# Block gates of two channel tiles in one run of products, and loaded tiles read later in the plan

## The chip, the cores and the metric

The kernel runs on one core of one Trainium2 chip. The metric is device time of one execution, in microseconds (us). Engines: TensorE (PE in the profile, its weight loads PEld) multiplies; VectorE (DVE), ScalarE (ACT) and GpSimd (POOL) work on elements; SyncE (SP) issues nearly all DMAs. Each engine takes its instructions in the order in which the program lists them.

## The reference

One encoder layer on 512 tokens of width 1024, in float32:

```python
h = rms_norm(x, g_pre) * (1 + scl) + shift            # scl, shift, gate from silu(c) @ w_c + b_c
xa, za, q, k, v, zb, ga, gb = split(h @ w_in)         # eight parts of 1024 columns
xa = centred_dwconv(xa, conv_w, conv_b)               # 4 taps along the sequence
h_fwd = rg_lru(xa, w_r_f, ...)                        # r, i = sigmoid(block_diag(xa)), 16 blocks of 64
h_bwd = rg_lru(xa, w_r_b, ..., reverse=True)          # linear recurrence along the sequence
y_a = ((h_fwd + h_bwd) * silu(za)) @ w_pa
y_b = (neighbourhood_attention(q, k, v, rpb) * silu(zb)) @ w_pb
merged = sigmoid(ga) * y_a + sigmoid(gb) * y_b
out = rms_norm(x + gate * (merged @ w_o), g_final)
```

## The kernel before

**Products.** A float32 product is made of three products of rounded parts: each operand is split into a high part (a cast on ACT, `whi`) and a remainder (a subtraction on DVE or POOL, `wlo`), and `mm3` (line 383) multiplies high by high, high by low and low by high into one PSUM bank. One output tile of 128 channels x 512 tokens is one call of `proj` (line 684): a 512 KB load `wraw` on SP, the cast `whi`, the subtraction `wlo`, and 8 steps of 3 matmuls, 24 in all. Here p*n* stands for the *n*-th of them; the list `main` keeps the first matmul of each, and a load is held back until p(*n*-5) has begun.

**Stages.** First the products for v, written out to a scratch in memory (`vscr`) and read back in pieces (`vt`). Then 8 pairs of heads, three products each (q, k, z), with the attention of a pair threaded between products: scores (`sp`), a bias step on DVE with a row minimum (`ttr`, line 799), exponentials on ACT (line 806), transposes on TensorE (`pt`, line 813), their split into parts (`pp`: ACT line 819, DVE line 821), the product with v (`pv`, line 829), and the combination of its parts (`vp`, `yt`: lines 838 to 844). Then four groups *g* of two channel tiles for the recurrent branch. Then eight merging products with `w_pa`, and the output product with `w_o` and the final norm.

**A group**, tiles 2g and 2g+1, is eight products: two for xa, two for za, two for ga, two with `w_pb`. After an xa product, `conv_gates` (line 930) makes the convolution `xc` (ACT, then three DVE steps), its parts `xh` and `xl`, and then the gates of this tile in one PE step, "gates" (line 954): 12 matmuls that use 64 rows of the array each, in 6 pairs, one pair member on the rows 0 to 63 and one on the rows 64 to 127, into four PSUM banks of class `gt`. ACT empties each bank in two halves (tanh, lines 960 and 963), DVE makes `ix` (line 968). `gate_a` (line 972) makes silu of za. `recur` (line 979) does the rest of the recurrence for both tiles and both directions: on ACT `dec` (line 986), `th` (line 988) and a square root (line 993), on DVE two products and a scan (lines 998 to 1005), the sum, the product with za, and the parts `yah`, `yal`, which the merging products read.

**Who sets the order.** Nothing is issued directly. `Plan.run` (line 258) is a list scheduler that runs when the kernel is built. Every `op` has a cost in us, a rank and its dependencies; the plan keeps a modelled time for each engine, and takes on each engine, among the steps that could begin within a small window of the earliest one (`WIN`, line 101), the one of lowest rank (line 280). It models the eight PSUM banks with a limit for each class (`LIMITS`, line 32), the tile slots in SBUF (36 of 512 columns, 32 of 1024) and the landing of DMAs (line 222). `late` (line 239) is added to the time at which a step's successors may begin in the plan. The order that comes out is the order of instructions on each engine; the planned times themselves are not kept. On the chip an engine whose next instruction has to wait holds up all that is behind it.

Of the kernel before, what the change touches and what calls it, by code (L numbers as in the profile page):

```python
# [28 lines left out]

NS, NW = 36, 32  # L30
WARM = 60
LIMITS = {"hx": 8, "acc": 3, "sp": 4, "pt": 2, "pv": 2, "mi": 2, "hd": 3, "gt": 4}


BLOCKS = [(0, 24, 8), (8, 32, 0), (24, 32, 0), (40, 24, 0)]
# [60 lines left out]
class Plan:  # L96
# [15 lines left out]
    def fixed(self, ap):  # L112
        return Tile_(None, ap=ap)

    def op(self, eng, cost, fn, rank, r=(), w=(), rw=(), lock=False, after=(), spare=0, size=0, until=None, late=0.0, hold=(), name=""):
        o = Op()
        o.alts = {eng: cost} if isinstance(eng, str) else dict(zip(eng, cost))
        o.fn, o.rank, o.lock, o.spare, o.size, o.name = fn, rank, lock, spare, size, name
        o.n, o.until, o.late = len(self.ops), until, late
        deps = set()  # L120
        for t in list(r) + list(rw):
            for f in t.family():
                deps.update(f.writers)
        for t in list(w) + list(rw):
            for f in t.family():
                deps.update(f.readers)
        for t in r:
            t.readers.append(o)
        for t in w:
            t.writers.append(o)  # L130
        for t in rw:
            for f in [t] + t.parts:
                f.writers, f.readers = [], []
            t.writers = [o]
        o.tiles = list(dict.fromkeys(t.base or t for t in list(w) + list(rw) + list(r) + list(hold)))
        for t in o.tiles:
            t.uses += 1
        o.data, o.succ, o.t = set(deps), [], 0.0
        deps.update(after)
        o.left = len(deps)  # L140
        for d in deps:
            d.succ.append(o)
        self.ops.append(o)
        return o
# [113 lines left out]
    def run(self):  # L258
        self.free = {e: 0.0 for e in self.ENG}
        self.dma, self.dve, self.pool = 0.0, 0.0, 0.0  # L260
        self.lanes = [0.0] * 8
        self.idle = [o for o in self.ops if o.until is not None]
        self.ready = {e: [] for e in self.ENG}
        for o in self.ops:
            if o.left == 0:
                self.enter(o)
        n = 0
        while n < len(self.ops):
            best = None
            for e in self.ENG:  # L270
                cand = []
                for _, _, o in self.ready[e][:40]:
                    s = self.est(o, e)
                    if s is not None and o.until is None:
                        cand.append((s, o))
                        if s <= self.free[e]:
                            break
                if cand:
                    lim = min(s for s, _ in cand) + self.WIN[e]
                    s, o = next(c for c in cand if c[0] <= lim)  # L280
                if self.idle and e == "PE":
                    f = self.idle[0]
                    fs = self.est(f, e)
                    if fs is not None and f.left == 0 and (not cand or fs + f.alts[e] <= s):
                        s, o, cand = fs, f, [f]
                if not cand:
                    continue
                if best is None or s < best[0]:
                    best = s, e, o
            if best is None:  # L290
                raise RuntimeError("nothing can begin: " + ", ".join(
                    f"{e}: {[(round(r, 2), o.name) for r, _, o in self.ready[e][:4]]}" for e in self.ENG))
            s, e, o = best
            for f in o.alts:
                self.ready[f].remove((o.rank, o.n, o))
            if self.idle and o is self.idle[0]:
                self.idle.pop(0)
            self.commit(o, e, s)
            n += 1
            if self.idle and o is self.idle[0].until:  # L300

                for d in self.idle:
                    self.ready[e].remove((d.rank, d.n, d))
                    self.leave(d)
                n += len(self.idle)
                self.idle = []
# [23 lines left out]
def layer(ctx, tc, x, x_t, par, w_m, w_g, bc_gate, w_v, w_in, w_blk, rpb, amask, w_pa, w_pb, w_o, g_final, out):  # L330
# [8 lines left out]
    def op(eng, cost, fn, rank, name="", **kw):  # L339
        return pl.op(eng, cost, fn, HEAD.get(name, rank), name=name, **kw)  # L340
# [27 lines left out]
    def load(t, dst, src, rank, size, after=(), spare=0, r=(), late=0.0, name="load"):  # L368

        return op("SP", 0.45, lambda e: nc.sync.dma_start(dst(), src() if callable(src) else src), rank,  # L370
                  r=r, w=[t], after=after, spare=spare, size=size, late=late, name=name)

    def cast(o, i):

# [306 lines left out]
    def gate_of(n, back):  # L681
        return [main[max(0, n - back)]] if n - back >= 0 else []

    def proj(w, rh, rl, lo="DVE"):

        n = len(main)
        raw, hi, low = W("wraw"), W("whi", F32R), W("wlo", F32R)
        v = lambda t: (lambda: t.ap.rearrange("p (k c) -> p k c", k=KD))
        load(raw, whole(raw), w, n - 5, 524288, after=gate_of(n, 5), spare=1,
             name=f"w{n}")  # L690
        op("ACT", act(1024), cast(whole(hi), whole(raw)), n - 2.2, r=[raw], w=[hi], after=gate_of(n, 3), name=f"whi{n}")
        engs = (lo,) if isinstance(lo, str) else lo
        costs = [dve(1024) if e == "DVE" else pool_(1024) for e in engs]
        op(engs, costs, sub(whole(low), whole(raw), whole(hi)), n - 2.1, r=[raw, hi], w=[low], lock=True, name=f"wlo{n}")
        o = B("acc")
        for k in range(KD):
            def f(e, k=k):
                mm3(o.ap, v(hi)()[:, k, :], v(low)()[:, k, :], rh[k][1](), rl[k][1](), k == 0, k == KD - 1)
            first = op("PE", pe(512, 3), f, 1000 + n + 0.01 * k, r=[hi, low, rh[k][0], rl[k][0]], rw=[o], name=f"p{n}")
            if k == 0:  # L700
                main.append(first)
        return n, o


# [50 lines left out]
    def attention(pr, q, k, z, nbt, pos):  # L755
# [24 lines left out]
        def half(bs):  # L780
# [79 lines left out]
        op("PE", 0.15, lambda e: nc.tensor.transpose(rcb.ap[:8, :P], rc.ap, ident.ap), pos - 0.3, r=[rc, ident], w=[rcb], name="rcb")  # L860
        op("ACT", 0.3, lambda e: nc.scalar.activation(rct.ap[:8, :P], rcb.ap[:8, :P], AF.Copy, scale=0.5), pos - 0.3, r=[rcb], w=[rct],
           name="rct")
        op("SP", 0.5, lambda e: nc.sync.dma_start(scr.ap, rct.ap[:8, :P]), pos - 3, r=[rct], w=[scr], size=4096, name="rcs")
        for h in range(2):
            src = bass.AP(scr.ap.tensor, scr.ap.offset + h * P, [[0, 64], [2 * P, 4], [1, P]])
            load(rcx, lambda h=h: rcx.ap[H[h], :].rearrange("p (b q) -> p b q", b=4), src, pos - 3, 131072, r=[scr], name="rcl", late=1.0)
# [60 lines left out]
        op("ACT", act(512), cast(whole(hi), whole(raw)), pos - 1, r=[raw], w=[hi], name="gwh")  # L927
        op("DVE", dve(512), sub(whole(lo), whole(raw), whole(hi)), pos - 1, r=[raw, hi], w=[lo], lock=True, name="gwl")

    def conv_gates(i, xa):  # L930
        n, o = xa
        xc = T("xc")
        op("ACT", act(512, 2), lambda e: nc.scalar.activation(xc.ap, o.ap, AF.Identity, bias=pc(64 + i, 65 + i),
# [8 lines left out]
        xh, xl = T("xh", F32R), T("xl", F32R)  # L942
        op("ACT", act(512), cast(whole(xh), whole(xc)), n, r=[xc], w=[xh], name="xh")
        op("DVE", dve(512), sub(whole(xl), whole(xc), whole(xh)), n, r=[xc, xh], w=[xl], lock=True, name="xl")
        g, c0 = gw[i // 2], (i % 2) * 256
        ri = [T("ri") for _ in range(4)]
        bks = [[B("gt"), B("gt")] for _ in range(2)]

        def f(e_):
            for d in range(2):  # L950
                for m, (w, xx) in enumerate(((g[0], xh), (g[0], xl), (g[1], xh))):
                    for e in range(2):
                        mm(bks[d][e].ap, w.ap[H[e], c0 + d * P:c0 + (d + 1) * P], xx.ap[H[e], :], m == 0, m == 2)
        op("PE", 1.55, f, n + 0.5, r=[g[0], g[1], xh, xl], w=bks[0] + bks[1], name="gates")
        for d in range(2):
            bk = bks[d]
            c = 16 * d + i
            for e in range(2):
                def f0(e_, e=e, d=d, bk=bk, c=c):
                    nc.scalar.activation(ri[2 * d].ap[H[e], :], bk[e].ap[H[e], :], AF.Tanh, bias=hb.ap[H[e], c:c + 1], scale=0.5)  # L960

                def f1(e_, e=e, d=d, bk=bk, c=c):
                    nc.scalar.activation(ri[2 * d + 1].ap[H[e], :], bk[e].ap[H[1 - e], :], AF.Tanh,
                                         bias=hb.ap[H[1 - e], c + 8:c + 9], scale=0.5)
                op("ACT", act(512, 1), f0, n + 0.3, r=[bk[e], hb], w=[ri[2 * d]], name="gr")
                op("ACT", act(512, 1), f1, n + 0.3, r=[bk[e], hb], w=[ri[2 * d + 1]], name="gi")
            u = ri[2 * d + 1]
            op("DVE", dve(512), lambda e, u=u: nc.vector.scalar_tensor_tensor(u.ap, u.ap, 1.0, xc.ap, op0=ALU.add, op1=ALU.mult),
               n + 0.6, r=[xc], rw=[u], lock=True, name="ix")
        st[i] = ri  # L970

    def gate_a(i, z):
        n, o = z
# [57 lines left out]
    for g in range(4):  # L1031
        tiles = (2 * g, 2 * g + 1)
        n0 = len(main)
        ybv = lambda: ([(ybh[k], whole(ybh[k])) for k in range(KD)], [(ybl[k], whole(ybl[k])) for k in range(KD)])
        load_gates(g, n0, gate_of(n0, 3))
        for i in tiles:
            conv_gates(i, proj(w_in[i], hhl, hll))
        for i in tiles:
            gate_a(i, proj(w_in[8 + i], hhl, hll))
        recur(tiles, n0 + 10)  # L1040
        for i in tiles:
            gate_m((i, 0), proj(w_in[48 + i], hhl, hll))
        for i in tiles:
# [241 lines left out]
```

## Time and profile before

| | |
|---|---|
| runs, us | 566.6, 566.64, 568.99; median 566.64 |
| the profiled execution | 569.44 us; its span, first to last instruction, 567.6 us; 1.84 us lie around it |
| mean granted clock of TensorE | 0.995 |
| ACT busy, DVE busy, POOL busy | 57%, 68%, 18% of the span |
| DMA | 83.47 MB, 147 GB/s on average |

The profile is of one execution, which was 2.8 us longer than the median of the runs. Times in it are us from the span's start; the durations of groups are means in ns. The busy time of PE is modelled from overlapping matmuls: one matmul of 512 columns shows some 0.39 us, while the next one starts 0.23 us after it. So what PE loses is read from the distance of starts, not from the busy share. The rows that the prediction works with stand in it.

### The profile page before, as it was taken

Reading aid. Unit: us, or ns where it says so; the run is one execution under the profiler, and the core shown is the slowest. Engines: PE = TensorE matmul, PEld = TensorE weight load, DVE = VectorE, ACT = ScalarE, POOL = GpSimd, SP = SyncE. Lnnn points to the kernel's source line nnn. Section 1 sums busy time; section 2 is a strip of 40 time slices with the busy share of each in tenths; the row PEclk is TensorE's granted clock in tenths of the full one; section 3 lists DMA queues with packets and bytes.
Section 4 is the critical chain, followed back from the end, with each engine's and each line's share of the span. In section 5 each row is a group of like instructions: output and inputs, shape, how many; then the busy total and the mean of one; then the engine's idle time right before and its main releaser. Section 6 shows DMA issues by size and latency. Waiting matters only on the chain.

```text
span 567.6 us, 7658 instructions
## 1 busy us (share of the span) xinstructions
PE 555.9 (98%) x2781; PEld 459.3 (81%) x2781; DVE 388.4 (68%) x696; ACT 322.4 (57%) x568; POOL 100.7 (18%) x95
## 2 busy tenths in 40 slices
PE   8999997999999999999999999999999999999995
PEld 8788886888888888887887887787788888888885
DVE  5899754665576667886489559749847996398323
ACT  6442545557466557579938867984894433234133
POOL 1103539184454550000000000000000000000220
PEclk9999998999999999999999999999999999999999
DMA  8993896652824721305222222223239813380002
GB/s 303 410 401 97 316 270 190 188 148 62 256 56 116 219 88 64 130 13 210 82 104 94 93 83 103 75 74 112 74 106 320 278 38 112 116 329 1 1 37 112
DMA packets 35580, 83.47 MB, mean 147 GB/s; under 512 B 3615, under 2 KB 10967, under 8 KB 35543
## 3 DMA queue, kind: packets, MB, share of 16 engines
q1 hardware_dynamic: 35264, 82.66, 44.1%
q8 instruction: 22, 0.36, 0.3%
q10 hardware_dynamic: 279, 0.32, 0.2%
q14 instruction: 15, 0.12, 0.1%
HBM read 76.65 MB, written 6.32 MB: 146 GB/s over the span
## 4 chain that ended last, share of the span: by engine, by line
PE 89%; DMA 7%; SPq 2%; DVE 1%; ACT 1%; issue 0%; ACTq 0%
PE acc L381 74%; PE hx L381 6%; DMA wv<-in_w_v_dram 3%; PE pv L381 3%; PE gt L381 2%; PE pt L813 2%; PE sp L381 2%; DMA vt<-vscr 2%; DMA wraw<-in_w_in_dram 1%; SPq L370 1%; DMA xT<-in_x_t_dram 1%; SPq L675 1%; DVE va L672 0%; DVE vl L378 0%; ACT vh L375 0%
## 5 line engine op out<-in xcount | busy, mean ns | idle before, releaser
L381 PE MATMUL acc<-hhl,whi 128*128 128x512 f32 x784 | 247.2, 396 | 0.0
L381 PEld LDWEIGHTS acc<-hhl,whi 128*128 128x128 f32 x784 | 143.8, 189 | 30.1 <-issue 1.8
L381 PE MATMUL acc<-hhl,wlo 128*128 128x512 f32 x392 | 153.5, 392 | 0.0
L381 PEld LDWEIGHTS acc<-hhl,wlo 128*128 128x128 f32 x392 | 73.9, 188 | 16.1
L375 ACT CAST whi<-wraw 128x1024 fp32r<-128x1024 f32 x72 | 74.2, 1045 | 9.1 <-DMA wraw<-in_w_in_dram 8.1
L378 POOL TENSOR_TENSOR wlo<-wraw,whi 128x1024 fp32r<-128x1024 f32 x23 | 56.5, 2457 | 73.2 <-ACT whi L375 39.0
L378 DVE TENSOR_TENSOR wlo<-wraw,whi 128x1024 fp32r<-128x1024 f32 x49 | 59.3, 1220 | 14.2 <-ACT whi L375 13.7
L1151 POOL TENSOR_TENSOR yo<-yo,gfin 128x512 f32<-128x512 f32 x6 | 8.2, 1360 | 338.0 <-ACT xr L1148 338.0
L381 PE MATMUL acc<-woh,mhl 128*128 128x512 f32 (+1 forms) x144 | 40.4, 365 | 0.0
L381 PE MATMUL acc<-yahl,whi 128*128 128x512 f32 x128 | 39.4, 389 | 0.0
L381 PE MATMUL acc<-ybhl,whi 128*128 128x512 f32 x128 | 39.4, 389 | 0.0
L1028 DVE SCALAR_TENSOR_TENSOR gm<-gm,acc 128x512 f32<-128x512 f32 x16 | 11.0, 688 | 39.4 <-PE acc L381 39.4
L799 DVE CUSTOM_DVE_ANT_0 p<-sp,nb 128x192 f32<-128x192 f32 (+1 forms) x64 | 32.7, 610 | 6.1 <-PE sp L381 6.1
L730 POOL TENSOR_TENSOR nb<-msk,braw 128x192 f32<-128x192 f32 (+1 forms) x48 | 29.0, 635 | 31.9 <-DMA braw<-in_rpb_dram 31.9
L381 PE MATMUL hx<-vh,hhl 128*128 128x512 f32 x112 | 33.7, 390 | 0.0
L806 ACT ACTIVATE p<-p,mn 128x192 f32<-128x192 f32 (+1 forms) x64 | 30.4, 478 | 5.1 <-DVE mn L799 5.0
L821 DVE TENSOR_TENSOR pp<-pt,pp 128x384 fp32r<-128x384 f32 (+1 forms) x32 | 19.8, 624 | 18.3 <-ACT pp L819 18.2
L381 PEld LDWEIGHTS acc<-woh,mhl 128*128 128x128 f32 x144 | 26.1, 189 | 4.4
L381 PEld LDWEIGHTS acc<-yahl,whi 128*128 128x128 f32 x128 | 24.0, 188 | 5.0
L381 PEld LDWEIGHTS acc<-ybhl,whi 128*128 128x128 f32 x128 | 24.0, 188 | 5.0
L381 PE MATMUL acc<-wol,mhl 128*128 128x512 f32 (+1 forms) x72 | 26.3, 365 | 0.0
L381 PE MATMUL acc<-yahl,wlo 128*128 128x512 f32 x64 | 24.9, 389 | 0.0
(202 smaller groups left out, 954.5 us busy)
## 6 DMA issues: line engine op xcount, KB each, us to landing
wraw<-in_w_in_dram SPq DMA_DIRECT2D x56, 512.0 KB, 5.8
wc<-in_w_m_dram SPq DMA_DIRECT2D x14, 512.0 KB, 9.6
vt<-vscr SPq DMA_DIRECT2D x24, 256.0 KB, 5.9
vscr<-va SPq DMA_DIRECT2D x8, 512.0 KB, 5.4
wraw<-in_w_pb_dram SPq DMA_DIRECT2D x8, 512.0 KB, 4.9
wraw<-in_w_pa_dram SPq DMA_DIRECT2D x8, 512.0 KB
wr<-in_w_g_dram SPq DMA_DIRECT2D x16, 256.0 KB, 5.8
wo<-in_w_o_dram SPq DMA_DIRECT2D x8, 512.0 KB, 4.1
```

What stands on the lines that cost most here:

```text
L370: return op("SP", 0.45, lambda e: nc.sync.dma_start(dst(), src() if callable(src) else src), rank, r=r, w=[t], after=after, spare=spare, s ...
L375: return lambda e: nc.scalar.copy(o(), i()) if e == "ACT" else nc.vector.tensor_copy(o(), i())
L378: return lambda e: ENGINE[e].tensor_tensor(o(), a(), b().bitcast(F32), op=ALU.subtract)
L381: nc.tensor.matmul(o, a, b, start=first, stop=last)
L675: op("SP", 0.6, lambda e: nc.sync.dma_start(dst, a.ap.bitcast(F32).rearrange("p (g c) -> p g c", g=2)), rank - 3, r=[a], w=[vscr[n]], size ...
L730: nc.gpsimd.tensor_tensor(o, mv, view, op=ALU.subtract)
L799: nc.vector.tensor_tensor_reduce(out=o, in0=v(spv(h, e)[:, :nk]), in1=v(nb[:, h, :nk]), scale=1.0, scalar=3e38, op0=ALU.add, op1=ALU.min, ...
L806: nc.scalar.activation(pv2(i), pv2(i), AF.Exp, bias=mn.ap[:, c:c + 1], scale=-1.0, accum_out=sm.ap[:, 2 * b + h:2 * b + h + 1])
L813: nc.tensor.transpose(ptp.ap[:, j * P:(j + 1) * P], pt_.ap[:, j * P:(j + 1) * P], ident.ap)
L821: op("DVE", dve(nt * P), lambda e_, ppv=ppv, pv4=pv4: nc.vector.tensor_tensor(ppv()[:, :, 1, :], pv4(), ppv()[:, :, 0, :].bitcast(F32), op ...
L1028: op("DVE", dve(512), lambda e: nc.vector.scalar_tensor_tensor(t.ap, t.ap, 1.0, o.ap, op0=ALU.add, op1=ALU.mult), n - 1.9, r=[o], rw=[t], ...
L1151: op(("DVE", "POOL"), (dve(w), pool_(w)), lambda e: ENGINE[e].tensor_tensor(y(), y(), gfin[n].ap[:, gs], op=ALU.mult), rank + 0.1, r=[gfin ...
```

## The change

There are two parts. **The gates:** `conv_gates` is cut in two. `conv` keeps the convolution and the parts `xh`, `xl`; `gates` makes the block products of both tiles of a group in four steps of 6 matmuls (tile by direction), the first of which waits for the parts of both tiles (`both`) and comes after the last matmul of the group's second za product has been placed (`ends[-1:]`), each of the others after the one before it. Their rank, `pos`, lies 2.5 above the number of the second xa product. The class `gt` may hold all eight banks instead of four, and a new field `wait` lets the second to fourth step be taken although another step could begin up to 0.4 us sooner. `recur` gets a rank 1.5 higher.

**The loads:** `load` gets `late` of 3 us (`SLACK`) for every load of a rank above 7.9 that has none of its own, and so does the store of the softmax sums (`rcs`). Ranks up to 7.9 belong to the products for v and to the first loads of the attention, so that those keep their plan. It changes no instruction and no wait; it changes the modelled time from which readers of those tiles are placed.

The diff, without the lines that only move or pass an argument:

```diff
+SLACK = 3
-LIMITS = {"hx": 8, "acc": 3, "sp": 4, "pt": 2, "pv": 2, "mi": 2, "hd": 3, "gt": 4}
+LIMITS = {"hx": 8, "acc": 3, "sp": 4, "pt": 2, "pv": 2, "mi": 2, "hd": 3, "gt": 8}
...
-                    s, o = next(c for c in cand if c[0] <= lim)
+                    s, o = next(c for c in cand if c[0] <= lim + c[1].wait)
...
-                  r=r, w=[t], after=after, spare=spare, size=size, late=late, name=name)
+                  r=r, w=[t], after=after, spare=spare, size=size, late=late or SLACK * (rank > 7.9), name=name)
...
+        ends.append(first)
         return n, o
...
-        op("SP", 0.5, lambda e: nc.sync.dma_start(scr.ap, rct.ap[:8, :P]), pos - 3, r=[rct], w=[scr], size=4096, name="rcs")
+        op("SP", 0.5, lambda e: nc.sync.dma_start(scr.ap, rct.ap[:8, :P]), pos - 3, r=[rct], w=[scr], size=4096, late=SLACK, name="rcs")
...
-        op("PE", 1.55, f, n + 0.5, r=[g[0], g[1], xh, xl], w=bks[0] + bks[1], name="gates")
...
-                op("ACT", act(512, 1), f0, n + 0.3, r=[bk[e], hb], w=[ri[2 * d]], name="gr")
-                op("ACT", act(512, 1), f1, n + 0.3, r=[bk[e], hb], w=[ri[2 * d + 1]], name="gi")
...
+    def gates(tiles, parts, begun):
+
+        pos = parts[1][0] + 2.5
+        g, n0 = gw[tiles[0] // 2], 0
+        both = [t for q in parts for t in q[2:4]]
+        for i, (n, xc, xh, xl, ri) in zip(tiles, parts):
+            c0 = (i % 2) * 256
             for d in range(2):
+                bk, c = [B("gt"), B("gt")], 16 * d + i
+
+                def f(e_, d=d, c0=c0, bk=bk, xh=xh, xl=xl):
+                    for m, (w, xx) in enumerate(((g[0], xh), (g[0], xl), (g[1], xh))):
+                        for e in range(2):
+                            mm(bk[e].ap, w.ap[H[e], c0 + d * P:c0 + (d + 1) * P], xx.ap[H[e], :], m == 0, m == 2)
+                o = op("PE", 0.69 if n0 else 1.09, f, pos, r=[g[0], g[1]] + both, w=bk, after=begun, wait=0.4 if n0 else 0.0, name="gates")
+                n0 += 1
+                begun = [o]
+                for e in range(2):
...
+                    op("ACT", act(512, 1), f0, pos - 0.2, r=[bk[e], hb], w=[ri[2 * d]], name="gr")
+                    op("ACT", act(512, 1), f1, pos - 0.2, r=[bk[e], hb], w=[ri[2 * d + 1].part()], name="gi")
...
         for i in tiles:
-            conv_gates(i, proj(w_in[i], hhl, hll))
+            parts.append(conv(i, proj(w_in[i], hhl, hll)))
         for i in tiles:
             gate_a(i, proj(w_in[8 + i], hhl, hll))
-        recur(tiles, n0 + 10)
+        gates(tiles, parts, ends[-1:])
+        recur(tiles, n0 + 11.5)
```

More of the change, by code (lines that the diff above doesn't have):

```diff
@@ L113, in fixed, with op @@
         return Tile_(None, ap=ap)
-    def op(self, eng, cost, fn, rank, r=(), w=(), rw=(), lock=False, after=(), spare=0, size=0, until=None, late=0.0, hold=(), name=""):
+    def op(self, eng, cost, fn, rank, r=(), w=(), rw=(), lock=False, after=(), spare=0, size=0, until=None, late=0.0, hold=(), wait=0.0, name=""):
         o = Op()
@@ L118, in op @@
         o.fn, o.rank, o.lock, o.spare, o.size, o.name = fn, rank, lock, spare, size, name
-        o.n, o.until, o.late = len(self.ops), until, late
+        o.n, o.until, o.late, o.wait = len(self.ops), until, late, wait
         deps = set()
@@ L682, in gate_of @@
         return [main[max(0, n - back)]] if n - back >= 0 else []
+    ends = []
     def proj(w, rh, rl, lo="DVE"):
@@ L928, in load_gates, with conv @@
         op("DVE", dve(512), sub(whole(lo), whole(raw), whole(hi)), pos - 1, r=[raw, hi], w=[lo], lock=True, name="gwl")
-    def conv_gates(i, xa):
+    def conv(i, xa):
         n, o = xa
@@ L944, in conv_gates @@
         op("DVE", dve(512), sub(whole(xl), whole(xc), whole(xh)), n, r=[xc, xh], w=[xl], lock=True, name="xl")
[L945 to L949, printed above, removed]
-            for d in range(2):
-                for m, (w, xx) in enumerate(((g[0], xh), (g[0], xl), (g[1], xh))):
-                    for e in range(2):
-                        mm(bks[d][e].ap, w.ap[H[e], c0 + d * P:c0 + (d + 1) * P], xx.ap[H[e], :], m == 0, m == 2)
@@ L954, in conv_gates @@
-        op("PE", 1.55, f, n + 0.5, r=[g[0], g[1], xh, xl], w=bks[0] + bks[1], name="gates")
[L955 to L964, printed above, removed]
-                op("ACT", act(512, 1), f0, n + 0.3, r=[bk[e], hb], w=[ri[2 * d]], name="gr")
-                op("ACT", act(512, 1), f1, n + 0.3, r=[bk[e], hb], w=[ri[2 * d + 1]], name="gi")
-            u = ri[2 * d + 1]
-            op("DVE", dve(512), lambda e, u=u: nc.vector.scalar_tensor_tensor(u.ap, u.ap, 1.0, xc.ap, op0=ALU.add, op1=ALU.mult),
-               n + 0.6, r=[xc], rw=[u], lock=True, name="ix")
@@ L970, in conv_gates, with f0, f1 @@
-        st[i] = ri
+        ri = st[i] = [T("ri") for _ in range(4)]
+        return n, xc, xh, xl, ri
+    def gates(tiles, parts, begun):
[4 more added lines that the diff above has]
+            c0 = (i % 2) * 256
+            for d in range(2):
+                bk, c = [B("gt"), B("gt")], 16 * d + i
[7 more added lines that the diff above has]
+                for e in range(2):
+                    def f0(e_, e=e, d=d, bk=bk, c=c, ri=ri):
+                        nc.scalar.activation(ri[2 * d].ap[H[e], :], bk[e].ap[H[e], :], AF.Tanh, bias=hb.ap[H[e], c:c + 1], scale=0.5)
+                    def f1(e_, e=e, d=d, bk=bk, c=c, ri=ri):
+                        nc.scalar.activation(ri[2 * d + 1].ap[H[e], :], bk[e].ap[H[1 - e], :], AF.Tanh,
+                                             bias=hb.ap[H[1 - e], c + 8:c + 9], scale=0.5)
+                    op("ACT", act(512, 1), f0, pos - 0.2, r=[bk[e], hb], w=[ri[2 * d]], name="gr")
+                    op("ACT", act(512, 1), f1, pos - 0.2, r=[bk[e], hb], w=[ri[2 * d + 1].part()], name="gi")
+                u = ri[2 * d + 1]
+                op("DVE", dve(512), lambda e, u=u, xc=xc: nc.vector.scalar_tensor_tensor(u.ap, u.ap, 1.0, xc.ap, op0=ALU.add, op1=ALU.mult),
+                   pos + 0.1, r=[xc], rw=[u], lock=True, name="ix")
@@ L1035, in layer @@
         load_gates(g, n0, gate_of(n0, 3))
+        parts = []
         for i in tiles:
-            conv_gates(i, proj(w_in[i], hhl, hll))
+            parts.append(conv(i, proj(w_in[i], hhl, hll)))
         for i in tiles:
             gate_a(i, proj(w_in[8 + i], hhl, hll))
-        recur(tiles, n0 + 10)
+        gates(tiles, parts, ends[-1:])
+        recur(tiles, n0 + 11.5)
         for i in tiles:
```

## The prediction, before the change was run

> **What bounds the kernel now.** I read the page first: its slices of granted clock and its chain of work.
>
> ```profile
> span 567.6 us, 7658 instructions
> ...
> PEclk9999998999999999999999999999999999999999
> ...
> PE 89%; DMA 7%; SPq 2%; DVE 1%; ACT 1%; issue 0%; ACTq 0%
> ```
>
> The chain that ends last is 89% TensorE. So only what takes time out of TensorE's own stream counts; the other engines matter where that stream waits for them. One slice shows a lower clock: the seventh, 85 to 99 us. Next the waits, TensorE alone, of which this is the longest:
>
> ```profile
> PE pv L381 <- DVE pp L821: 3.2, 1, 3.2
> ```
>
> It happened once. The timeline of TensorE there, and the sums by stretch:
>
> ```profile
> 83.20 0.93 PE L813 MATMUL pt<-ident,p 128*128 128x128 f32 x7
> ...
> 85.82 0.39 PE L381 MATMUL acc<-hhl,wlo 128*128 128x512 f32 x1
> 89.39 0.74 PE L381 MATMUL pv<-pp,vt 128*128 128x256 f32 x4 [3.19 <-DVE pp L821]
> ```
>
> ```profile
> 85.80:89.40 3.60, 0.41 (x3) 0.01 (x1) 0.62 (x2) 2.55 (x5) 3.60 (x6) 1.00 0.71 230
> 89.40:91.40 2.00, 2.00 (x12) 1.77 (x13) 1.43 (x4) 1.95 (x7) 1.89 (x3) 0.85 0.46 140
> 91.40:94.40 3.00, 3.00 (x9) 2.40 (x8) 2.30 (x6) 1.39 (x3) 2.55 (x2) 0.53 0.13 26
> ```
>
> Columns of the second fence: stretch, length, busy time of PE, PEld, DVE, ACT and POOL, then the granted clock, the DMA share and GB/s. The transposes of 83.20 are done, their parts `pp` are not, and TensorE stands until 89.39. Afterwards it is granted 0.85 and then 0.53 of its clock. Why `pp` is late stands in ACT's timeline:
>
> ```profile
> 81.44 0.19 ACT L806 ACTIVATION_READ_ACCUMULATOR p<-p,mn 128x1 f32 x1
> 86.80 1.05 ACT L375 CAST whi<-wraw 128x1024 fp32r<-128x1024 f32 x1 [5.17 <-DMA wraw<-in_w_in_dram]
> 87.87 0.37 ACT L838 COPY vp<-pv 64x256 f32<-64x256 f32 x1
> 88.27 0.97 ACT L819 CAST pp<-pt 128x384 fp32r<-128x384 f32 x2
> ```
>
> and in the chain of waits, in order of time:
>
> ```profile
> 79.76 6.97 DMA wraw<-in_w_in_dram
> ```
>
> ACT stands 5.17 us before a weight cast whose load lands at 86.73, and the two `pp` casts that TensorE wants are queued behind it. That cast feeds p14, which begins much later (row below). So it is the planned order, not the work, that costs this time: the plan believed the load to be there sooner.
>
> **The loads, term by term.** The stall: a 512-column matmul is followed by the next one 0.23 us after its start (rows below), so TensorE was free at 85.82 + 0.23 = 86.05, and lost 89.39 - 86.05 = 3.34 us. The clock behind it: 2.00 x (1 - 0.85) + 3.00 x (1 - 0.53) = 0.30 + 1.41 = 1.71 us. Together 5.05 us.
>
> The Trainium skill (TensorE: Matmul & The Clock Gate, Part 1) says that the clock falls to half after an idle window of about 3.4 us, and that the window runs freely. By that rule an idle time of this length may lose the clock or keep it from one execution to the next, and one clearly shorter always keeps it: the 1.71 us would be 0 or so in some executions. The 0.53 agrees; that it varies no run here shows.
>
> With 3 us added in the plan, the cast of p14 is placed from 3 us after its planned landing. Its planned place was between 81.63, where ACT came free (81.44 + 0.19), and 86.80. From 81.63 + 3.0 = 84.6 on it stands behind the `pp` casts, which can begin at about 83.20 + 0.93 = 84.13. That margin is 0.5 us, and I don't have the planned times: this is the weakest link, and the first rival below. If it holds, ACT makes `pp` at 84.1 to 85.1 instead of 88.27 to 89.24, DVE follows within the time that TensorE has products until 86.05, and both terms go. Late next would be p14:
>
> ```profile
> 88.31 2.37 POOL L378 TENSOR_TENSOR wlo<-wraw,whi 128x1024 fp32r<-128x1024 f32 x1
> ```
>
> ```profile
> 98.60 0.39 PE L381 MATMUL acc<-hh,whi 128*128 128x512 f32 x1
> ```
>
> Its remainder is ready at 88.31 + 2.37 = 90.68, and p14, which began at 98.60, would begin 5.05 us sooner at 93.55: 2.9 us of cover. If that cover were gone (another load later by more than that), TensorE would wait for the excess, at most the 3.34 us over again. SP's queue only gains: the `rcs` store, whose readers move, sits there behind the attention that now ends earlier. Elsewhere I cost the later readers at nothing: the waits name no other stall of TensorE after 90 us, and loads are released five products, some 27 us, ahead of their product. The bound for a stall that the new order makes anew is the one that the old order had, 5.05 us; I keep it for the rivals.
>
> **The gates, term by term.** TensorE around one "gates" step:
>
> ```profile
> 262.65 0.39 PE L381 MATMUL acc<-hhl,wlo 128*128 128x512 f32 x1
> 262.88 0.61 PE L381 MATMUL acc<-hhl,whi 128*128 128x512 f32 x2
> 263.33 0.39 PE L381 MATMUL acc<-hhl,wlo 128*128 128x512 f32 x1
> 263.65 0.50 PE L381 MATMUL gt<-xh,gwh 64*128 64x512 f32 x2
> ...
> 264.91 0.40 PE L381 MATMUL gt<-xh,gwl 64*128 64x512 f32 x2
> 265.24 0.73 PE L381 MATMUL acc<-hhl,whi 128*128 128x512 f32 x2
> 265.81 0.39 PE L381 MATMUL acc<-hhl,wlo 128*128 128x512 f32 x1
> ```
>
> Three matmuls take 263.33 - 262.65 = 0.68 us, 0.227 each. From 263.33 to 265.81 stand one matmul, six pairs (each pair runs at once, in the time of one) and two matmuls: 9 x 0.227 = 2.04 us. It took 2.48. So going into the 64-row form and out of it costs 0.44 us a time. There are eight such steps; the change makes four runs of two, removes four entries and exits, and keeps all 96 matmuls: 4 x 0.44 = 1.76 us. I take 1.7. The bounds are 0 (each run split by a product in the plan) and 1.76.
>
> What the run asks for: eight banks, each read by two tanh.
>
> ```profile
> L960 ACT ACTIVATE ri<-gt,hb x32: 667/684/687, 253.8 to 412.3; 64x512 f32<-64x512 f32 x32
> L963 ACT ACTIVATE ri<-gt,hb x32: 680/684/689, 254.5 to 413.0; 64x512 f32<-64x512 f32 x32
> ```
>
> A tanh takes 0.684, 0.70 from start to start (rows below), so one bank is free after 1.40 us and all eight after 16 x 0.70 = 11.2 us. The first of the four steps is done about 0.95 us into the run, its first bank is free at 0.95 + 0.2 + 1.4 = 2.6 us, and the next product wants it at 0.44 + 12 x 0.227 = 3.2 us. The last two gate banks are found at 2.3 us: six of the seven others hold the earlier steps, and the eighth, of the za product, has had its tanh and its DVE step. So there is 0.6 us of cover, gone if ACT makes the za tanh first or sits in a weight cast.
>
> The first step now also waits for the parts of the second tile, with all later products queued behind it. In the last group:
>
> ```profile
> 402.44 0.62 ACT L375 CAST xh<-xc 128x512 fp32r<-128x512 f32 x1
> ...
> 406.00 0.81 ACT L986 ACTIVATE dec<-ri,sp4n 128x512 f32<-128x512 f32 x1
> 407.66 0.60 ACT L975 ACTIVATE za<-acc 128x512 f32<-128x512 f32 x1 [0.85 <-PE acc L381]
> ...
> 413.04 0.68 ACT L963 ACTIVATE ri<-gt,hb 64x512 f32<-64x512 f32 x1
> ```
>
> That `xh` came at 402.44 because the tanh of the tile before stood ahead of it; those move behind it. The run begins where the za product ends, about 406. So no wait there.
>
> **The sum.** For the profiled execution: 569.44 - 5.05 - 1.7 = 562.7 us. The median of the runs, 566.64, lies 2.80 lower than it, and one run lies at 568.99. I take it that this difference is mostly the 1.71 us of lost clock, which the median run then doesn't have, so that only the stall goes from it: 566.64 - 3.34 - 1.7 = 561.6. If the median does have it, it is 566.64 - 6.75 = 559.9. Forecast 561.6; this case by itself spans 559.9 to 562.7.
>
> **The rivals.** *The stall stays or comes back.* The cast moves by 3.0 where ACT stood 5.17 us; if the plan had placed it early, it still precedes `pp`, or a different load holds up ACT in the same busy stretch (DMA share 0.71 to 0.97 there). Then only the gates count: 566.64 - 1.7 = 564.9. For it: the 0.5 us of margin. Against: a cast placed much earlier would have run in an earlier gap.
>
> *The banks.* If ACT has the za tanh (0.60) or a cast (1.05) in front, the product behind each run waits 0.4 to 1.0 us; four times 0.43 takes the gain of the gates back, and the result is 561.6 + 1.7 = 563.3, at worst 561.6 + 4 x 1.0 = 565.6. This is the rule that speaks against the change: the Trainium skill (TensorEngine Tiling (Array Packing), PSUM Bottleneck) says that packing speeds up TensorE and not the emptying of PSUM, which may then be the bound. By the page this would be the likely outcome; the 2.6 against 3.2 us above doesn't bear it out, and no run here has such a run of products.
>
> *The change doesn't do what it says.* The plan splits the runs, and the order by the stall is as it was: 566.6.
>
> *Slower: the last recurrence is late.* The merging products read the last tile's `yal` and have little time for it:
>
> ```profile
> 447.06 0.68 DVE L378 TENSOR_TENSOR yahl<-ri,yahl 128x512 fp32r<-128x512 f32 x1
> ```
>
> ```profile
> 450.31 0.61 PE L381 MATMUL acc<-yahl,whi 128*128 128x512 f32 x2
> 450.76 0.39 PE L381 MATMUL acc<-yahl,wlo 128*128 128x512 f32 x1
> 450.99 0.39 PE L381 MATMUL acc<-hh,whi 128*128 128x512 f32 x1
> ```
>
> Ready at 447.74, wanted at 450.31: 2.6 us. Now the last tanh ends at about 407.0 + 11.2 + 0.6 = 418.8 instead of 413.72, 5.1 us later; the three steps of tile 6 that ACT had already done by 406.8 (0.81 each) are behind it, 2.4 us; and the higher rank lets one more weight cast and one more subtraction pass, about 1.2 us. That is 8.7 us. TensorE would wait 8.7 - 2.6 = 6.1 us and lose 1.71 us of clock: 561.6 + 7.8 = 569.4, 0.5% slower. It makes the kernel slower from a shift of 5.9 us on. Against it: the product at 450.99 doesn't read `yal`, lasts 24 x 0.227 = 5.4 us, and the plan can put it first, which covers shifts up to 8 us; and DVE and ACT have idle time there.
>
> **How the numbers follow.** Both parts hold: 0.58. The stall stays or returns: 0.18. The banks: 0.08. Not what it says: 0.06. Late recurrence, or a new stall of its size: 0.10. The range takes in both readings of the median and what is left when the stall stays or nothing happens: 559.5 to 566.8; outside lie the late recurrence and part of the first case's low side. A measurement of this kernel can tell about 0.5% from no change, that is 563.8 and 569.5. Faster by more: the first case and half of the banks, 0.62. Slower by more: 0.09. The same: 0.29.
>
> **What would show it.** Right: no wait of TensorE for `pp` near 86 us and a clock of 1.00 from 85 to 95; the cast behind the two `pp` casts in ACT's timeline; four runs of 24 gate matmuls, with 0.32 us steps only at their two ends, and the product behind each run at the usual distance. Wrong: a wait of TensorE for a tanh (banks), for `yahl` (recurrence) or again for `pp`; gate matmuls in more than four places; or a span near 563 us with a median near 567, which would mean that the median runs never had the stall.

## The result

| | before | after |
|---|---|---|
| median, us (runs) | 567.12 (5) | 562.78 (5) |
| lowest to highest | 566.6 to 569.61 | 562.54 to 562.86 |
| the profiled execution; its span | 569.44; 567.6 | 562.54; 560.4 |

The ratio is 0.9917, 95% interval 0.9892 to 0.9941: faster by 0.8%, clear of the 0.5% that can be told apart. The median fell by 4.34 us, the profiled executions differ by 6.90. And the runs, 3 us apart before, lie within 0.32 us after. Ratios, here and below, leave out one execution of `slack1`, which took 931.33 us at a mean clock of 0.558, where all others have 0.987 or more.

The page after (granted clock, chain):

```profile
PEclk9999999999999999999999999999999999999998
...
PE 99%; DVE 0%; POOL 0%; issue 0%; ACT 0%; POOLq 0%
```

The lower clock in the seventh slice is gone, and the chain that ends last is now TensorE throughout. The waits of TensorE name one thing only, from the start of the kernel:

```profile
PE hx L501 <- POOL epsc L449: 1.5, 1, 1.5
```

The stretches of the old stall, in the same columns as before (length; PE, PEld, DVE, ACT, POOL; clock; DMA share; GB/s):

```profile
85.80:89.40 3.60, 3.60 (x21) 2.87 (x19) 2.82 (x6) 3.49 (x7) 3.54 (x4) 1.00 0.85 228
89.40:91.40 2.00, 2.00 (x15) 1.82 (x14) 0.04 (x1) 0.90 (x3) 1.95 (x3) 1.00 0.86 239
91.40:94.40 3.00, 3.00 (x15) 2.49 (x14) 2.16 (x5) 2.02 (x3) 3.00 (x2) 1.00 0.97 225
```

TensorE is busy all through, at full clock, while DMA is busier than it was before (0.85 to 0.97, as against 0.71, 0.46 and 0.13). ACT's timeline shows why:

```profile
82.70 0.48 ACT L824 CAST pp<-pt 128x384 fp32r<-128x384 f32 x1
83.07 1.05 ACT L377 CAST whi<-wraw 128x1024 fp32r<-128x1024 f32 x1
84.02 0.59 ACT L824 CAST pp<-pt 128x512 fp32r<-128x512 f32 x1
...
87.00 1.04 ACT L377 CAST whi<-wraw 128x1024 fp32r<-128x1024 f32 x1
```

The late weight cast now runs at 87.00, behind both `pp` casts. An earlier weight cast, that of p14, has taken a place between them; its load had landed, so it waits for nothing. The gates of the last group, TensorE:

```profile
396.80 0.39 PE L383 MATMUL acc<-hhl,wlo 128*128 128x512 f32 x1
397.12 0.50 PE L383 MATMUL gt<-xh,gwh 64*128 64x512 f32 x2
...
400.09 0.50 PE L383 MATMUL acc<-hh,whi 128*128 128x512 f32 x1
400.42 0.40 PE L383 MATMUL acc<-hl,whi 128*128 128x512 f32 x1
```

From 396.80 to 400.42 stand one matmul, twelve pairs and one matmul, 14 x 0.227 = 3.18 us; it took 3.62. One entry and exit for the whole run: 0.44 us, where there were two. All four groups look like this.

### The profile page after: what moved, and what is told of

It is laid out like the page before. It is cut to its first block, busy times and chain, and to the rows that moved or that the text cites. A ratio compares the mean times of both kernels' runs of the same rounds, so it can differ in the third digit from the quotient of the medians.

```text
span 560.4 us, 7670 instructions
## 1 busy us (share of the span) xinstructions
PE 552.5 (99%) x2781; PEld 459.2 (82%) x2781; DVE 386.9 (69%) x696; ACT 324.5 (58%) x568; POOL 100.1 (18%) x95
## 4 chain that ended last, share of the span: by engine, by line
PE 99%; DVE 0%; POOL 0%; issue 0%; ACT 0%; POOLq 0%
PE acc L383 78%; PE hx L383 8%; PE pv L383 3%; PE sp L383 2%; PE pt L818 2%; PE gt L383 2%; PE hx L501 1%; PE hx L434 1%; PE hd L548 0%; PE hd L493 0%; PE hd L510 0%; PE mi L383 0%; PE mi L865 0%; DVE yo L1185 0%; DVE yo L1153 0%
## 5 line engine op out<-in xcount | busy, mean ns | idle before, releaser
L804 DVE CUSTOM_DVE_ANT_0 p<-sp,nb 128x192 f32<-128x192 f32 (+1 forms) x64 | 31.2, 616 | 16.7 <-PE sp L383 13.7
L945 DVE SCALAR_TENSOR_TENSOR xc<-acc,prm,xc 128x511 f32<-128x511 f32 (+1 forms) x24 | 18.0, 748 | 13.7 <-ACT xc L938 13.2
```

The source lines that it names most:

```text
L804: nc.vector.tensor_tensor_reduce(out=o, in0=v(spv(h, e)[:, :nk]), in1=v(nb[:, h, :nk]), scale=1.0, scalar=3e38, op0=ALU.add, op1=ALU.min, ...
L945: nc.vector.scalar_tensor_tensor(a, b, wcol, a, op0=ALU.mult, op1=ALU.add)
```

## The experiments

The theory: the second part acts through one place in ACT's order, the weight cast ahead of the `pp` casts; the first saves four times what TensorE pays for going into the 64-row form and out of it. The rivals: later readers help everywhere a little; the gain of the gates is something else than this switch; and, for the difference between 4.34 and 6.90 us, that the lost clock comes and goes between executions, or that the stall itself has different lengths. Every run is compared with runs of the kernel before in the same batch, on the same chip; their medians were 567.33, 568.96 and 567.68 in the three batches, the second of which (`split16`, `stall10`, `stall14`, `stall20`) ran on another chip than the other two. The change itself was not run again beside them: 562.78 is its median above.

**Each part alone.** Gates in runs, loads planned as before:

```diff
-SLACK = 3
+SLACK = 0
```

> The gates in runs, the loads planned as before (SLACK = 0). If the two parts are separate, as the prediction has it: the wait of TensorE for pp near 86 us is there again, some 3.3 us with a lower clock behind it, four runs of 24 gate matmuls, and the span is 560.4 + 5.05 = 565.5 us or so in a profile that has the lost clock, the time 565 to 568, with runs that differ by 2 to 3 us as those of before did. If the run of gates alone had moved the order in such a way that the stall goes, it is 562.8 with a small spread.

Ratio 0.9984, interval 0.9964 to 1.0003; 565.07 to 568.26 us over 12 executions. Its profile, TensorE first, then ACT:

```profile
84.98 0.39 PE L383 MATMUL acc<-hhl,wlo 128*128 128x512 f32 x1
87.29 0.74 PE L383 MATMUL pv<-pp,vt 128*128 128x256 f32 x4 [1.93 <-DVE pp L826]
```

```profile
84.70 1.05 ACT L377 CAST whi<-wraw 128x1024 fp32r<-128x1024 f32 x1 [3.88 <-DMA wraw<-in_w_in_dram]
85.78 0.37 ACT L843 COPY vp<-pv 64x256 f32<-64x256 f32 x1
86.17 0.97 ACT L824 CAST pp<-pt 128x384 fp32r<-128x384 f32 x2
```

The stall is there, in the same place and for the same reason. But it is shorter: 87.29 - 84.98 - 0.23 = 2.08 us, as ACT waited 3.88 us for the load and not 5.17, and this execution, of 565.07 us, kept its clock (0.998 on average). Each execution lists its mean clock. Four of the twelve lie at 565.07 to 565.48 with 0.998 or 0.999, one at 566.39; the other seven at 567.41 to 568.26 with 0.990 to 0.995. Up to the gates this kernel's order on TensorE is that of the kernel before, so that it shows the same stall, with the clock kept in some executions and lost in others. The 1.7 us of the gates are less than the difference between the two kinds, and so this part alone does not show in the median; the lowest executions differ by 1.3 us (565.07 against 566.39).

Loads 3 us later, gates as before (the first part's edits undone):

> The loads planned 3 us later, the gates as before in eight steps. Separate parts: no wait of TensorE for pp, clock 1.00 from 85 to 95 us, and 562.8 + 4 x 0.41 = 564.4 us, with runs as close together as those after. If the spread of the runs of before comes from elsewhere than from the stall, the spread stays 2 to 3 us here.

564.1 us (563.88 to 564.47), ratio 0.9927, interval 0.9903 to 0.9952. The stall is gone and with it the spread. Against the whole change it lacks 1.3 us by the medians and 1.9 by the profiled executions, about what the gates should give. So the two parts are separate, and the second one also takes away the spread.

**One load, and less slack.** The 3 us only for the load of p15:

```diff
-... late=late or SLACK * (rank > 7.9), name=name)
+... late=late or SLACK * (name == "w15"), name=name)
```

and none for `rcs`.

> The gates in runs, and 3 us later in the plan for the reader of one single load, that of the product whose cast stood ahead of the pp casts (p15 by the order of the casts). In ACT's order that one cast moves behind them and little else changes. If this place is the whole effect of the second part: 562.8 us, no wait of TensorE for pp. If the later readers elsewhere matter too: between 563.5 and 566.

563.18 us over four executions (562.16 to 564.56), ratio 0.9912, interval 0.9879 to 0.9944. ACT, at the place in question:

```profile
83.75 0.97 ACT L824 CAST pp<-pt 128x384 fp32r<-128x384 f32 x2
...
87.20 1.05 ACT L377 CAST whi<-wraw 128x1024 fp32r<-128x1024 f32 x1
```

One cast moved gives the gain of the second part, within the measurement. A smaller wait of 1.0 us for an exponential, near 102 us, was in its profile and not in that of the full change; so the later readers elsewhere may do a little, too, which four executions don't show.

`SLACK = 1`:

> The change with SLACK = 1 instead of 3. In the order of ACT's instructions the weight cast that waited still stands ahead of the two pp casts. The theory that this one place makes the stall: the wait of TensorE for pp is back, time 565 to 568. The rival, that later readers everywhere take away many small waits in proportion to the slack: about a third of the gain, some 566, without one long wait.

Ratio 0.9997, interval 0.9977 to 1.0017. With 1 us the cast keeps its place ahead of the `pp` casts, and TensorE waits for `pp` again, 1.9 us in the profile. It is not a share of the slack that counts but whether this cast changes places.

**More slack.** `SLACK = 6`:

> The change with SLACK = 6. In ACT's order the late cast stands far behind the pp casts, as with 3. If that place is what counts, 562.8 us again. If readers placed too late cost something of their own, slower, with a wait of TensorE for a weight cast or its remainder.

575.27 us, ratio 1.0118, interval 1.0089 to 1.0148: slower than the kernel before. The cast in question is behind the `pp` casts, and TensorE waits for `pp` in other places, 8.2 us in three waits. One of them, in the timelines of TensorE, DVE and SP:

```profile
149.47 0.39 PE L383 MATMUL acc<-hhl,wlo 128*128 128x512 f32 x1
152.99 1.17 PE L383 MATMUL pv<-pp,vt 128*128 128x256 f32 x4 [3.13 <-DVE pp L826]
```

```profile
149.34 0.69 DVE L872 TENSOR_TENSOR sz<-sz,rcx 128x512 f32<-128x512 f32 x1 [4.88 <-DMA rcx<-rscr]
```

```profile
131.92 5.84 SPq L372 DMA_DIRECT2D vt<-vscr  x8
137.82 1.06 SPq L372 DMA_DIRECT2D wraw<-in_w_in_dram  x2
139.32 1.46 SPq L372 DMA_DIRECT2D rcx<-rscr  x2
```

The readers of the softmax sums (`rcx`) move with the slack as well: SP issues ten other DMAs from 131.92 on before theirs, DVE comes to the product with `rcx` and waits 4.88 us for it, with the remainder steps of `pp` behind it. The other two waits have the same product in front of them, where DVE waits 2.63 and 5.81 us. It is the first stall again, with another load on another engine.

**The switch.** The four gate steps of a group put apart, each behind every second step of the first ga product: 16 runs of 6 matmuls. The main lines:

```diff
-        gates(tiles, parts, ends[-1:])
+        ga = [proj(w_in[48 + i], hhl, hll) for i in tiles]
+        gates(tiles, parts, steps[-16:-8:2])   # step j after matmul group 2j of the first ga product
```

> The change with its four gate steps of a group apart: each behind another pair of steps of the first ga product, so that there are 16 runs of 6 gate matmuls instead of 4 runs of 24, and the same matmuls. If the gain of the run is the going in and out of the 64-row form, 0.42 us a time: 12 more of them, 5.0 us, 567.8 us. If a large part of what the eight steps of before cost was something else (a wait for banks or for the parts of the tile), the time grows by clearly less, under 566.

567.53 us, 4.75 more than the change, 0.40 for each of the 12 more runs. One of them:

```profile
401.66 0.39 PE L383 MATMUL acc<-hh,wlo 128*128 128x512 f32 x1
401.98 0.50 PE L383 MATMUL gt<-xh,gwh 64*128 64x512 f32 x2
402.31 0.40 PE L383 MATMUL gt<-xl,gwh 64*128 64x512 f32 x2
402.55 0.40 PE L383 MATMUL gt<-xh,gwl 64*128 64x512 f32 x2
402.87 0.73 PE L383 MATMUL acc<-hhl,whi 128*128 128x512 f32 x2
403.45 0.39 PE L383 MATMUL acc<-hhl,wlo 128*128 128x512 f32 x1
```

The steps into the run, after its first pair, out of it and after the next matmul are 0.32 to 0.34 us; the rest are 0.23. Nothing waits for a bank or an operand here, so the switch is the whole price, and the gain of the gates is shown to be it, 1.6 to 1.8 us for the four runs fewer. (`loads_only` lacks 1.3 by the medians; why it is not the full 1.6 there is open.)

**The cover of the banks.** The tanh of the second za tile made five times, which the plan doesn't know:

```diff
-lambda e: nc.scalar.activation(t.ap, o.ap, AF.Tanh, scale=0.5)
+lambda e: [nc.scalar.activation(t.ap, o.ap, AF.Tanh, scale=0.5) for _ in range(1 + 4 * (i % 2))]
```

> The tanh of the second za tile of each group made five times instead of once, which the plan doesn't know: ACT comes to the gate tanh some 1.7 us later. By the prediction's account of the banks (0.6 us of cover for the bank of the next product, about as much for the last two gate banks), TensorE waits some 1.1 to 1.4 us in or behind each of the four runs of products: 562.8 + 4 to 6 us, 567 to 569. If the banks have far more room than that, it costs nothing.

573.57 us, 10.8 more than the change. TensorE and ACT in the first group, then the stretches behind the first two runs of products:

```profile
258.89 0.39 PE L383 MATMUL gt<-xh,gwh 64*128 64x512 f32 x1
260.70 0.50 PE L383 MATMUL gt<-xh,gwh 64*128 64x512 f32 x1 [1.42 <-DVE za L987]
```

```profile
256.81 3.12 ACT L986 ACTIVATE za<-acc 128x512 f32<-128x512 f32 x5 [2.86 <-PE acc L383]
```

```profile
261.00:265.00 4.00, 4.00 (x14) 2.89 (x11) 0.69 (x1) 3.86 (x7) 0.00 (x0) 0.61 0.00 0
311.00:315.00 4.00, 4.00 (x19) 3.07 (x20) 3.97 (x6) 3.87 (x7) 0.00 (x0) 1.00 0.00 0
```

The last of the four steps waits for the za bank, 260.70 - 258.89 - 0.23 = 1.58 us in each group, 6.3 in all. One tanh takes 0.60 us and the five take 3.12, so the extra ones take 2.5 us, and about 0.9 us of it was covered. I had expected 1.1 to 1.4 us each and a lower total: I took the extra tanh for 1.7 us, and left out that the clock can go as well. In this execution it was 0.61 over the 4 us behind the first of the four waits and 0.59 behind the third, and stayed at 1.00 behind the other two. The waits and two losses of 1.7 us make 9.7 us; the rest of the 10.8 is not accounted for.

**Stalls of a set length.** One `pp` cast of the third pair of heads is repeated N times, which the plan doesn't know; the wait hangs on no DMA.

```diff
+                more = N * (pr == 2 and edge and members is groups[1])
-... lambda e_, ppv=ppv, pv4=pv4: nc.scalar.copy(ppv()[:, :, 0, :], pv4()),
+... [nc.scalar.copy(ppv()[:, :, 0, :], pv4()) for _ in range(1 + more)],
```

> The change with ten extra copies (the same pp cast repeated) ahead of one pp cast of the third pair of heads, which the plan knows nothing of: a wait of TensorE of a set length, about 10 x 0.37 - 1.8 = 1.9 us, that hangs on no DMA. By the clock theory with a window of some 3.4 us: no loss of clock, 562.8 + 1.9 = 564.7 us, small spread. If shorter idle times can cost the clock too: some executions 1.5 to 2.5 us longer with a lower mean clock.

> The same with fourteen copies: a wait of about 3.4 us. By the free-running window: some executions keep the clock, 566.2 us, others lose it, 567.9, and the mean clock of each execution tells which. If the length of the stall by itself decided, all would be alike.

> The same with twenty copies: a wait of about 5.6 us. The clock is lost in every execution: 562.8 + 5.6 + 1.7 = 570.1 us, a clock near 0.5 for some 3 us behind it.

> Seven extra copies ahead of one pp cast in the changed kernel. The runs with ten, fourteen and twenty gave idle times of 3.31, 5.35 and 8.43 us, 0.51 us for each copy, so that seven should give 3.31 - 3 x 0.51 = 1.8 us. If the length of the idle time decides about the clock, nothing is lost at this length: 562.8 + 1.8 = 564.6 us in all executions. If its place in a window that runs freely decides at every length: some executions near 566.3 with a lower mean clock.

> Nine extra copies: an idle time of 2.8 us, between the 2.1 us of the profile that kept its clock and the 3.35 us of the one that lost it. Length alone: either all executions at 565.6 or all near 567.3. Phase: a mixture of the two.

| copies | idle in the profile, us | times, us | over 562.78 (median) | mean clocks |
|---|---|---|---|---|
| 7 | 1.80 | 564.33 to 565.15 | 2.0 | 0.996, 0.997 |
| 9 | 2.82 | 565.59 to 568.62 | 4.2 | 0.991 to 0.999 |
| 10 | 3.31 | 567.13 to 569.0 | 5.0 | 0.991 to 0.996 |
| 14 | 5.35 | 569.74 to 571.46 | 7.6 | 0.990 to 0.996 |
| 20 | 8.43 | 572.92 to 574.08 | 10.6 | 0.987 to 0.993 |

The idle time is the distance of starts less 0.23 us, here for seven and for nine copies:

```profile
130.34 0.39 PE L383 MATMUL acc<-hhl,wlo 128*128 128x512 f32 x1
132.37 0.74 PE L383 MATMUL pv<-pp,vt 128*128 128x256 f32 x4 [1.64 <-DVE pp L827]
```

```profile
130.66 0.39 PE L383 MATMUL acc<-hhl,wlo 128*128 128x512 f32 x1
133.71 0.58 PE L383 MATMUL pv<-pp,vt 128*128 128x256 f32 x1 [2.66 <-DVE pp L827]
```

My estimate of the first three lengths was 1.4 to 2.8 us too short: a copy costs 0.51 us, not 0.37, so the run meant for 1.9 us had 3.3. What follows: at this place 1.80 us never cost the clock, with 3.31 every execution lay at least 1.0 us above the sum of both, half of them 1.7 or more, and at 2.82, one length in one program, the executions differ by 3 us, from none lost to more than the idle time itself. So length and execution both decide.

What differs between executions can be read from the clock in the traces. First the kernel before, then `stall9`, in the columns of above:

```profile
87.40:90.81 3.41, 1.42 (x9) 1.19 (x10) 1.47 (x4) 3.34 (x10) 3.35 (x4) 1.00 0.53 162
90.81:94.22 3.41, 3.41 (x13) 2.83 (x11) 2.89 (x6) 1.95 (x4) 2.90 (x3) 0.50 0.13 41
94.22:97.63 3.41, 3.41 (x20) 2.97 (x19) 0.65 (x2) 1.04 (x3) 3.41 (x7) 1.00 0.99 251
```

```profile
129.67:133.08 3.41, 1.38 (x7) 0.80 (x5) 0.00 (x0) 3.22 (x8) 1.07 (x3) 1.00 0.00 0
133.08:136.50 3.42, 2.79 (x9) 2.40 (x10) 3.12 (x8) 3.36 (x8) 0.00 (x0) 0.50 0.00 0
136.50:139.91 3.41, 3.41 (x13) 2.72 (x12) 1.05 (x2) 0.85 (x2) 3.29 (x3) 0.50 0.05 8
```

The clock is at 0.50 for 3.41 us, or for twice that, and full on both sides. Where one trace has two such stretches, their starts lie whole multiples of 3.413 us apart: 153.08 and 200.87 in `slack6` 14 of them, 261.89 and 360.88 in `za_more` 29. So each of these executions is cut into windows of 3.413 us, and the low clock begins with a window.

Before, 1.99 us of the stall's idle time fell into the window from 87.40 to 90.81, and the next one was at 0.50, which is the 1.71 us lost. In `stall9` 2.19 us fell into the window up to 133.08, the next one had 0.63 us of idle time as well, and the low clock lasted for two: hence more than the idle time itself. In `gates_only` the 2.08 us of the stall were split at 86.54 into 1.33 and 0.75, and the clock stayed. Of the four waits of `za_more` the first and the third lay whole in one window, and the other two were split.

Over the waits of all traces, after the first 20 us, the clock went where 1.58 us or more fell into one window, and stayed where it was 1.50 or less (`stall7`: 1.50 and 0.30). The 1.58 us stand within 64-row products; between full products the least that cost the clock was 1.99. That the executions without a trace differ in the same way is argued, not shown.

The Trainium skill (TensorE: Matmul & The Clock Gate, Part 1) gives an idle window of about 3.4 us as what costs the clock. The length of the window agrees, 3.413 us; that the window is idle throughout does not, as 1.99 and 2.19 us of it were enough here, and 1.58 us twice behind the gates. The measurement decides: waits well under 3.4 us are not safe.

## Why the prediction was right

**The stall and its place.** Right. The term for the profiled execution was 5.05 us and the sum 562.7, against 562.54 measured. The products' starts show the term itself: ahead of the stall TensorE began p12 at 78.96 before and 78.54 after, behind it p15 at 105.87 and 100.37, so 5.08 us went in between. The late cast went behind the `pp` casts. The weakest link, 0.5 us of margin, held. I had not seen that, with every load later, the cast ahead of it would move too and fill the gap; but the link doesn't need this, as in `one_load` that cast stays at 76.38 us and the late one is behind `pp` all the same. With 1 us of slack the link fails.

**The product that the cast feeds.** Wrong by one. By the order of the casts in the program it is p15's and not p14's. Its cover was larger than the 2.9 us that I gave; nothing else hung on it.

**The clock and the median.** The choice, that the median execution of before mostly kept its clock, fits the runs of the prediction (in the later batches executions of 566.4 to 567.0 us have mean clocks of 0.996 to 0.998), and it is why the gain in the median is smaller than in the profiles. The mis-sized term is the stall in those executions: I took the 3.34 us of the profile, and in the two traces of this stall with the clock kept it is 2.08 us (`gates_only`, 565.07 us, 2.3 over the change) and 2.05 (`slack1`). With the first, 566.64 - 2.08 - 1.7 = 562.9, against 562.78; my 561.6 was 1.2 us low. No execution of the kernel before that kept its clock was traced, so this size is carried over from those two. How often the clock goes is not fixed: in the batch with median 568.96, on the other chip, 22 of 30 executions of the kernel before lie over 568 us with clocks of 0.992 to 0.996, so the gain in medians would be near 1.1% there, by an estimate from 562.78 against 568.96. That the load lands earlier or later is seen in two profiles, of two kernels with the same order up to there (ACT's waits of 5.17 and 3.88 us); why it does is open.

**The gates.** Right: 1.76 at most, 1.7 taken. The runs stayed whole, and the switch is 0.40 to 0.44 us by two ways of measuring.

**The banks.** The account held, with more room at the last two gate banks than the working's 0.6 us. ACT, last group, after:

```profile
397.23 0.60 ACT L986 ACTIVATE za<-acc 128x512 f32<-128x512 f32 x1 [4.17 <-PE acc L383]
398.12 0.69 ACT L972 ACTIVATE ri<-gt,hb 64x512 f32<-64x512 f32 x1 [0.30 <-PE gt L383]
398.82 0.69 ACT L975 ACTIVATE ri<-gt,hb 64x512 f32<-64x512 f32 x1
```

The first bank, which by the working is the next product's (the trace does not number the banks), is read by 398.82 + 0.69 = 399.51, and the next product begins at 400.09: 0.58 us, as against the 0.6 of the working. By the Trainium skill (TensorEngine Tiling (Array Packing), PSUM Bottleneck) the emptying of PSUM may become the bound; in this trace it does not, though the room is only 0.6 us here and 0.9 us at the za bank (`za_more`).

**The late recurrence.** The mechanism is real and did not cost anything, for the reason given against it. The last `yal`, DVE, and TensorE around it:

```profile
445.27 0.69 DVE L380 TENSOR_TENSOR yahl<-ri,yahl 128x512 fp32r<-128x512 f32 x1
```

```profile
442.40 0.39 PE L383 MATMUL acc<-hh,whi 128*128 128x512 f32 x1
...
447.84 0.61 PE L383 MATMUL acc<-yahl,whi 128*128 128x512 f32 x2
```

It is ready at 445.96. In the old order, with the last two steps of the merging product from 442.40 on, TensorE would have wanted it in the second of them, at 442.40 + 0.68 = 443.08, and waited 2.9 us. The plan has put the next ga product in between, from 442.40 to 447.84, and goes on with the last two steps of the merging product after it.

## What to carry to other kernels

Where a plan orders in-order engines, look for the queue in which one instruction waits for a DMA while work that TensorE wants stands behind it: moving that one instruction is the gain, and a margin on all loads is only a way of doing so, that with 1 us did nothing and with 6 us made the same stall elsewhere. A stall has two prices, its length and the clock behind it; the second depends on where the stall falls in the clock's windows, and so comes and goes between executions: compare runs by their spread and clock, too. Products in a partial-row form cost some 0.4 us for each time of going into the form and out of it, so collect them, as far as the banks and the engine that empties them allow.

## What the runs showed of the hardware that was not expected

A wait of 2.82 us in one trace, made to be the same in every execution, cost between nothing and more than its own length (565.59 to 568.62 us over 12 executions). The low clock came in whole windows of 3.413 us, and what counted in the traces was how much of a wait fell into one window: 1.99 us between full products cost it, 1.50 did not. And 1.58 us of idle time within a run of 64-row products cost the clock in two places of four (0.61 and 0.59 over the next 4 us), those where it lay whole in one window; a wait of 1.80 us between full products never did in six executions. Whether the kind of products ahead of the wait moves the bound was not tried.
